# Score products of four tiles at a time in an attention stage, and three smaller moves, in a hybrid decoder block

## The chip, the cores and the metric

One Trainium2 chip, one of its cores. The metric is the device time of one execution in microseconds; the median over the runs is compared. Engines are named as in the profile: PE is TensorE's matmuls, PEld its weight loads, DVE is VectorE, ACT is ScalarE, POOL is GpSimd, SP is SyncE, whose queue issues most of the DMAs.

## What is computed

One decoder block on 1024 positions of width 1024, in float32:

```python
h = x + 0.5 * swiglu(rms_norm(x, g1), w1, w3, w2)               # D_FF = 2816
u = rms_norm(h, g)
proj = u @ w_in                       # q, k, v (3 x 768), pool input (512), two gates (2 x 1024)
# A: 12 heads of 64 in three groups, (window, dilation) = (128,1), (512,4), (2048,16):
#    causal banded attention on each residue class, blocks of 128 queries against
#    the block before and the own one; the three groups mixed by their softmax denominators
y_attn = dilated_mixture_attention(q, k, v) @ w_branch_attn
# B: trailing means over 2/4/8/16 positions minus the token, a 128x128 map per group
y_pool = multiscale_pool(pz, pool_w, pool_scale) @ w_branch_pool
h = h + (sigmoid(gA) * y_attn + sigmoid(gB) * y_pool) @ w_out
h = h + 0.5 * swiglu(rms_norm(h, g2), ...)
return rms_norm(h, final_norm)
```

## The kernel before

**Number format.** Every operand of a matmul is split in a high part (a copy on ACT, rounded to fp32r) and a low part (the difference, on DVE or POOL). A product is three matmuls: high by high, high by low, low by high (the helper `three`). The large products use a scheme of seven products for eight (`ORDER` is 1, 6, 2, 7, 5, 4, 3); the bank of product 5 is read out once and then product 3 is accumulated into it.

**Stages.** First FFN up (to about 440 us of the span), first FFN down (`Down`, to about 650), the input projection (`items`, to 1035), attention with the pool branch's product in between (1035 to about 1154), merge and output projection, second FFN up, second FFN down. In most stages the order of the instructions on each engine is the order in which the program is written (`manual_schedule`): an engine's queue is served in that order, and an instruction that waits holds up those behind it.

**Down.** 42 steps: seven products `m`, each over six pieces `s` of the inner dimension (five of two tiles, one of one). A step of two tiles is 24 matmuls (L814). Step i loads the left sums of step i + 3 (`load`, L753) and prepares the operands of step i + 2 (`begin`: `bhi`, `ahi` on ACT at L767, `blo`, `alo` on DVE or POOL at L771). Weight pieces come through a `Stream` in a fixed order (L76): a piece is loaded as soon as its place is free, and none can overtake another. Six pieces (`APART`) have places of their own, two buffers in the pool of the down stage; a piece of these is loaded when fewer than two of them are held. They are pieces 13 and 14, 22 and 23, 37 and 38 of each down product.

**Input projection.** One item k is one of the seven products of one `Mix`. In iteration k the program writes: the eviction of the item before if that was product 1 or 5; the operands of item k + 2; the product of item k (L331); the eviction of the item before if it was another product; then one step of each job in `later` that is due: rotation, turning of values, splitting of late weights, and for the two pool mixes `window` (shifted sums L1188, splits `pd_hi`, `pd_lo` at L1192 and L1193, the product `pm` at L1200 and its eviction). Evictions are at L1084 (product 1), L1091 (7), L1095 (5), L1098 (4), L1101 (3).

**Attention.** There are N = 48 slots: two pairs of heads, three groups, eight query tiles each; `slots[s]` has one or two key blocks (`blocks`). The loop runs over q, two slots each. PSUM has eight banks under two tags, "mm" and "acc", four each. A slot's scores take two "mm" banks, one for each head; the two heads' matmuls use the two halves of the rows (64x128 weights, written `64*128` in the profile) and run side by side. One step q is, in the order of the program:

- `scores(2q)` and `scores(2q+1)`: 12 matmuls, L1624
- `trans_p(q-1)`: 4, 6 or 8 transposes of the exponents, `tp`, L1671; one "acc" bank for up to 512 columns, two for more
- one or two groups of four matmuls of the pool branch (`next(fill)`, `yp`, L1763); three groups make one "acc" bank
- `values(q-2)`: 6, 9 or 12 matmuls, `o`, L1704, one "acc" bank
- DVE: `gather(q-3)` (copies of `o`, L1727), `masked` (score minus mask with a running minimum, L1642)
- the split of step q - 1's transposes: `ehi` on ACT (L1683), `elo` on DVE (L1686)
- in two steps of four, the splits of the next group's q and k (`split_ring`, ACT L1266, POOL L1267)
- `end_branches`: a finished `yp` bank times its gate, on DVE (L1777)
- `exponents` on ACT (L1651)
- `house`: among other things the factors of the first pair of heads (steps 16, 17) and `combine` for it, two advances a step in steps 18 to 21: a step of it is four transposes into an "mm" bank (`factor_rows`, `fa`, L1605), the product on DVE (L1736), the sum on POOL (L1738); the last one is ACT's copy `att` and POOL's difference.

Behind the loop come the last transposes, `ehi` and `elo`, the last values, the factors of the second pair of heads (`factors[1]`) and its `combine`.

Of the kernel before, what the change touches and what calls it, by code (L numbers as in the profile page):

```python
# [16 lines left out]
P = 128  # L17
# [8 lines left out]
HD = 64  # L26
# [20 lines left out]
class Stream:  # L47


    def __init__(self, nc, pool):  # L50
        self.nc, self.pool = nc, pool
        self.pieces, self.tiles = [], {}
        self.depth = self.n_loaded = self.n_used = self.n_back = self.end = 0
        self.apart, self.n_apart = set(), 0

    def room(self):
        if self.n_loaded in self.apart:
            return self.n_apart < 2
        return self.n_loaded - self.n_apart < self.n_back + self.depth

    def load(self):
# [76 lines left out]
def tile_block(  # L138
# [585 lines left out]
    class Down:  # L724
# [3 lines left out]
        def __init__(self, name, sums, half_tile, pair):  # L728
            self.name, self.sums, self.half_tile = name, sums, half_tile

            self.parts = pair.parts(self.place)
            self.steps = [(m, s) for m in range(len(DOWN)) for s in range(len(PAIRS))]
            self.held, self.g, self.ops, self.banks = {}, {}, {}, {}
            self.n_lo = 0
            self.last_shared = len(self.steps) - (2 if name == "f1" else len(PAIRS))
            self.right, self.apart = {}, set()
            downs.append(self)

        def size(self, i):
            js = PAIRS[self.steps[i][1]]  # L740
# [80 lines left out]
        def run(self, pool, after, tick=None):  # L821
            def half_tile(tag, n):
                return pool.tile([P, HALF], F32, tag=tag, bufs=4, name=f"{tag}_{self.name}{n}")

            self.half_tile = half_tile
            n = len(self.steps)
            done = []
            for i, (m, s) in enumerate(self.steps):
                if i < n - 2:
                    for t in range(4):  # L830
                        self.multiply(i, t)
                if i == n - 1:
# [12 lines left out]
                if s == len(PAIRS) - 1:  # L845
                    done = [(m, t) for t in range(4)]
                self.ops.pop(i - 1, None)
                if m == len(DOWN) - 1 and tick is None:
                    raws.depth = max(3, len(PAIRS) + 1 - s)
                if i == 1:  # L850
                    next(self.parts, None)
                if i + 3 < n:
                    self.load(i + 3)
                if i + 2 < n and not ahead:
                    self.begin(i + 2)
                if i in (0, 2):
                    next(self.parts, None)
                if tick is not None:
                    tick(i)
# [554 lines left out]
    with tc.manual_schedule():  # L1414
# [4 lines left out]
        for k in range(len(items) + 4):  # L1419
# [12 lines left out]
            if k - 1 in results:  # L1432
                q, m = items[k - 1]
                mixes[q].out(m, results.pop(k - 1))
                if m == 3:
                    later.append([k, mixes[q].finish()])
            for job in list(later):
                if job[0] <= k:
                    wait = next(job[1], 0)
                    job[0] = k + wait  # L1440
                    if not wait:
                        later.remove(job)
# [168 lines left out]

    T = {}

    def scores(s):
        hp, g, i = slots[s]
        u = hp * GROUPS + g
        n = blocks(g, i)
        ks = slice((i + 1 - n) * P, (i + 1) * P)
        ps = [bank("mm", f"s{s}_{a}")[:, :n * P] for a in range(2)]
        (qhi, qlo, _), (khi, klo, _) = ring[u]  # L1620
        for j, (l, r) in enumerate(three((qhi, qlo), (khi, klo))):
            for a in range(2):
                rows = slice(a * HD, (a + 1) * HD)
                pe.matmul(ps[a], l[rows, i * P:(i + 1) * P], r[rows, ks], start=(j == 0), stop=(j == 2))  # L1624
        T[s] = {"s": ps}

    def masked(s):
        hp, g, i = slots[s]
# [214 lines left out]
    def house(s):  # L1843
# [7 lines left out]
            get_stats(*slots[s - 5][:2])  # L1851
        if N // 2 + 8 <= s < N // 2 + 11:
            advance(factors[0])
        if N // 2 + 12 <= s < N // 2 + 20:
            advance(combines[0][(s - N // 2 - 12) // 4])
        if N - 32 <= s < N - 13:
            advance(first)
        if s in (N - 6, N - 5, N - 4):
# [3 lines left out]
    with tc.manual_schedule():  # L1862
# [7 lines left out]
        splits = {}  # L1870
        for q in range(N // 2):
            send()
            scores(2 * q)
            scores(2 * q + 1)
            if q == 0:
                advance(fill, 2)
            if q > 0:
                trans_p(q - 1)
                splits[q - 1] = split_p(q - 1)
                next(fill, None)  # L1880
                if q % 4 != 3:
                    next(fill, None)
            if q > 1:
                values(q - 2)
# [24 lines left out]
        load_merge(1)  # L1909
        open_w_o()  # L1910
        q = N // 2
        trans_p(q - 1)
        splits[q - 1] = split_p(q - 1)
        advance(factors[1])
# [421 lines left out]
```

## Time and profile before

| | |
|---|---|
| median of 3 runs (lowest to highest) | 1901.11 us (1900.65 to 1902.72) |
| the profiled execution | 1900.85 us, its span 1899.1 us |
| mean granted TensorE clock | 0.999 |
| attention, 1035 to 1154 us | PE 117.88 of 119.00 us busy, DVE 96.56, ACT 81.00, POOL 48.65 |

A group's row reads: line, engine, operation, tiles written <- read, shape, count, then busy time, mean duration in ns, idle time before it and what ended that. A timeline row reads: start in us, duration in us, engine, line, operation, tiles, count, and in brackets the engine's idle time before it with what ended it. A matmul's duration runs until its result is written, and the next starts long before that; so the distance of two starts says how fast matmuls follow each other, not the duration.

### The profile page before, as it was taken

Reading aid. Unit: us, or ns where it says so; the run is one execution under the profiler, and the core shown is the slowest. Engines: PE = TensorE matmul, PEld = TensorE weight load, DVE = VectorE, ACT = ScalarE, POOL = GpSimd, SP = SyncE. Lnnn points to the kernel's source line nnn. Section 1 sums busy time; section 2 is a strip of 40 time slices with the busy share of each in tenths; the row PEclk is TensorE's granted clock in tenths of the full one; section 3 lists DMA queues with packets and bytes.
Section 4 is the critical chain, followed back from the end, with each engine's and each line's share of the span. In section 5 each row is a group of like instructions: output and inputs, shape, how many; then the busy total and the mean of one; then the engine's idle time right before and its main releaser. Section 6 shows DMA issues by size and latency. Waiting matters only on the chain. (4 is left out here: it accounts for less than half of the span.)

```text
span 1899.1 us, 24689 instructions
## 1 busy us (share of the span) xinstructions
PE 1884.7 (99%) x8822; PEld 1563.3 (82%) x8822; DVE 1337.4 (70%) x1975; ACT 773.6 (41%) x1394; POOL 718.7 (38%) x533
## 2 busy tenths in 40 slices
PE   9999999999999999999999999999999999999998
PEld 8888888888788888888888888888888888888886
DVE  6776556557886777658886787787665566577867
ACT  7323323333434543334445762363333323334344
POOL 5433333331323354445545456543333333313221
PEclk9999999999999999999999999999999999999999
DMA  5254223336465526765578968644432223354654
GB/s 190 62 199 162 84 89 116 128 117 230 148 228 204 183 89 217 239 213 196 207 254 307 314 212 282 267 153 150 143 127 105 84 103 119 134 197 156 224 195 144
DMA packets 144019, 330.78 MB, mean 174 GB/s; under 512 B 17560, under 2 KB 39064, under 8 KB 142360
## 3 DMA queue, kind: packets, MB, share of 16 engines
q1 hardware_dynamic: 140152, 318.36, 48.6%
q10 hardware_dynamic: 3744, 10.85, 1.5%
q8 instruction: 69, 1.13, 0.2%
q14 instruction: 54, 0.44, 0.1%
HBM read 229.61 MB, written 99.55 MB: 173 GB/s over the span
## 5 line engine op out<-in xcount | busy, mean ns | idle before, releaser
L814 PE MATMUL d_f<-bhi_f,alo_f 128*128 128x512 f32 x616 | 240.1, 390 | 1.4 <-POOL alo_f L771 1.2
L814 PE MATMUL d_f<-bhi_f,ahi_f 128*128 128x512 f32 x616 | 240.3, 390 | 0.0
L814 PE MATMUL d_f<-blo_f,ahi_f 128*128 128x512 f32 x616 | 239.7, 389 | 0.0
L771 POOL TENSOR_TENSOR alo_f<-g_f,ahi_f 128x512 fp32r<-128x512 f32 x60 | 90.0, 1516 | 268.1 <-ACT ahi_f L767 268.1
L331 PE MATMUL u_mixm<-xhi_t_mix,wc_mixm 128*128 128x512 f32 x608 | 157.7, 391 | 0.1
L814 PEld LDWEIGHTS d_f<-bhi_f,alo_f 128*128 128x128 f32 x616 | 115.6, 188 | 26.5 <-POOL alo_f L771 2.6
L814 PEld LDWEIGHTS d_f<-bhi_f,ahi_f 128*128 128x128 f32 x616 | 115.6, 188 | 24.2 <-ACT h L415 0.5
L814 PEld LDWEIGHTS d_f<-blo_f,ahi_f 128*128 128x128 f32 x616 | 115.6, 188 | 23.9
L331 PEld LDWEIGHTS u_mixm<-xhi_t_mix,wc_mixm 128*128 128x128 f32 x608 | 113.4, 188 | 24.0 <-ACT wc_mixm L319 0.6
L331 PE MATMUL u_mixm<-xhi_b_mix,wc_mixm 128*128 128x512 f32 x456 | 120.4, 392 | 0.5 <-DVE y_m L1095 0.5
L322 POOL TENSOR_TENSOR wc_mixm<-s_mixm,wc_mixm 128x512 fp32r<-128x512 f32 x52 | 78.1, 1503 | 109.8 <-ACT wc_mixm L319 103.9
L331 PEld LDWEIGHTS u_mixm<-xhi_b_mix,wc_mixm 128*128 128x128 f32 x456 | 84.8, 188 | 18.1 <-issue 0.9
L319 ACT ACTIVATE wc_mixm<-s_mixm 128x512 fp32r<-128x512 f32 x76 | 47.0, 628 | 110.8 <-DVE s_mixm L373 53.6
L767 ACT ACTIVATE ahi_f<-g_f 128x1024 fp32r<-128x1024 f32 x84 | 81.9, 975 | 11.5 <-DMA g_f<-gs_f 11.5
L331 PE MATMUL u_mixm<-xlo_t_mix,wc_mixm 128*128 128x512 f32 x304 | 81.3, 389 | 0.0
L322 POOL TENSOR_TENSOR wc_mixm<-raw,wc_mixm 128x512 fp32r<-128x512 f32 x40 | 59.3, 1484 | 43.1 <-ACT wc_mixm L319 35.4
L2016 PE MATMUL wo<-w_o,o_hi 128*128 128x512 f32 x224 | 69.3, 390 | 0.0
L767 ACT ACTIVATE bhi_f<-s_f2w 128x512 fp32r<-128x512 f32 x55 | 32.9, 627 | 86.0 <-DVE s_f2w L789 67.1
L767 ACT ACTIVATE bhi_f<-s_f1w 128x512 fp32r<-128x512 f32 x55 | 33.1, 629 | 83.2 <-DVE s_f1w L789 69.9
L331 PEld LDWEIGHTS u_mixm<-xlo_t_mix,wc_mixm 128*128 128x128 f32 x304 | 57.1, 188 | 12.0
L771 DVE TENSOR_TENSOR alo_f<-g_f,ahi_f 128x1024 fp32r<-128x1024 f32 (+1 forms) x48 | 59.7, 1244 | 8.3 <-ACT ahi_f L767 8.3
L331 PE MATMUL u_mixm<-xlo_b_mix,wc_mixm 128*128 128x512 f32 x228 | 61.0, 389 | 0.0
(1332 smaller groups left out, 4758.9 us busy)
## 6 DMA issues: line engine op xcount, KB each, us to landing
g_f<-gs_f SPq DMA_DIRECT2D x70, 512.0 KB
gs_f<-y_f SPq DMA_DIRECT2D x88, 256.0 KB
raw<-in_w2a_dram SPq DMA_DIRECT2D x35, 512.0 KB
raw<-in_w2b_dram SPq DMA_DIRECT2D x35, 512.0 KB
gs_f<-gb_f SPq DMA_DIRECT2D x46, 256.0 KB
raw<-in_w1a_dram SPq DMA_DIRECT2D x22, 512.0 KB
raw<-in_w3a_dram SPq DMA_DIRECT2D x22, 512.0 KB
raw<-in_w1b_dram SPq DMA_DIRECT2D x22, 512.0 KB
```

Source lines behind the costliest of these rows:

```text
L319: ac.activation(w[:, 0], src, AF.Copy)
L322: eng.tensor_tensor(w[:, 1], src, w[:, 0].bitcast(F32), op=OP.subtract)
L331: pe.matmul(p, a, b, start=(start and n == 0), stop=(n == 11), skip_group_check=not start)
L767: ac.activation(hi[:, c], src, AF.Copy)
L771: eng.tensor_tensor(lo[:, d], src[:, o], hi[:, d].bitcast(F32), op=OP.subtract)
L814: pe.matmul(self.banks[m][t], l, r, start=(first and q == 0), stop=(last and q == 2))
L2016: pe.matmul(banks[m][t], l, r, start=(st == 0 and j == 0 and q == 0), stop=(st == 1 and j == 1 and q == 2))
```

## The change

Four things, none of which alters an operand.

- A step's two slots share two score banks: head a of both slots in bank a, the second slot from column 256 on. `scores(q)` now does both slots, and even steps call it for q and q + 1 (24 matmuls), odd steps not at all. Odd steps begin with a group of `yp` ahead of the transposes, and of the groups behind the transposes the second is kept only where q mod 4 is 1; step 0 has one group instead of two. The number of groups up to the end of the loop stays 42.
- `combine` of the first pair of heads moves from the ends of steps 18 to 21 to the beginnings of the odd steps 19, 21 and 23 and to the place right behind the loop, two advances each.
- A step of `window` that would fall on an iteration whose item is product 5 is put off to the next iteration.
- The extra places of the weight stream are none at first; step 8 of a down product opens two, and loads.

```diff
     def room(self):
         if self.n_loaded in self.apart:
-            return self.n_apart < 2
+            return self.n_apart < self.places
...
             downs.append(self)
+            raws.places = 0
...
                 if i + 3 < n:
                     self.load(i + 3)
+                if i == len(PAIRS) + 2:
+                    raws.places = 2
+                    raws.load()
                 if i + 2 < n and not ahead:
                     self.begin(i + 2)
...
-                    later.append([k, mixes[q].finish()])
+                    later.append([k, mixes[q].finish(), mixes[q].kind])
             for job in list(later):
-                if job[0] <= k:
+                if job[0] <= k and not (job[-1] == "pool" and k < len(items) and items[k][1] == 5):
...
-    def scores(s):
-        hp, g, i = slots[s]
-        u = hp * GROUPS + g
-        n = blocks(g, i)
-        ks = slice((i + 1 - n) * P, (i + 1) * P)
-        ps = [bank("mm", f"s{s}_{a}")[:, :n * P] for a in range(2)]
-        (qhi, qlo, _), (khi, klo, _) = ring[u]
-        for j, (l, r) in enumerate(three((qhi, qlo), (khi, klo))):
-            for a in range(2):
-                rows = slice(a * HD, (a + 1) * HD)
-                pe.matmul(ps[a], l[rows, i * P:(i + 1) * P], r[rows, ks], start=(j == 0), stop=(j == 2))
-        T[s] = {"s": ps}
+    def scores(q):
+        banks = [bank("mm", f"s{q}_{a}") for a in range(2)]
+        for s in (2 * q, 2 * q + 1):
+            hp, g, i = slots[s]
+            n = blocks(g, i)
+            ks = slice((i + 1 - n) * P, (i + 1) * P)
+            c0 = s % 2 * 2 * P
+            ps = [b[:, c0:c0 + n * P] for b in banks]
+            (qhi, qlo, _), (khi, klo, _) = ring[hp * GROUPS + g]
+            for j, (l, r) in enumerate(three((qhi, qlo), (khi, klo))):
+                for a in range(2):
+                    rows = slice(a * HD, (a + 1) * HD)
+                    pe.matmul(ps[a], l[rows, i * P:(i + 1) * P], r[rows, ks], start=(j == 0), stop=(j == 2))
+            T[s] = {"s": ps}
...
-        if N // 2 + 12 <= s < N // 2 + 20:
-            advance(combines[0][(s - N // 2 - 12) // 4])
...
             send()
-            scores(2 * q)
-            scores(2 * q + 1)
-            if q == 0:
-                advance(fill, 2)
+            if q % 2 == 0:
+                scores(q)
+                scores(q + 1)
+            elif N // 4 + 7 <= q:
+                advance(combines[0][(q - N // 4 - 7) // 4], 2)
+            if q == 0 or q % 2 == 1:
+                next(fill, None)
             if q > 0:
                 trans_p(q - 1)
                 splits[q - 1] = split_p(q - 1)
                 next(fill, None)
-                if q % 4 != 3:
+                if q % 4 == 1:
                     next(fill, None)
...
         q = N // 2
+        advance(combines[0][1], 2)
         trans_p(q - 1)
```

More of the change, by code (lines that the diff above doesn't have):

```diff
@@ L53, in __init__ @@
         self.depth = self.n_loaded = self.n_used = self.n_back = self.end = 0
-        self.apart, self.n_apart = set(), 0
+        self.apart, self.n_apart, self.places = set(), 0, 0
     def room(self):
         if self.n_loaded in self.apart:
-            return self.n_apart < 2
+            return self.n_apart < self.places
         return self.n_loaded - self.n_apart < self.n_back + self.depth
```

## The prediction

> **What bounds the kernel now.** I read the page first.
>
> ```profile
> span 1899.1 us, 24689 instructions
> PE 1884.7 (99%) x8822; PEld 1563.3 (82%) x8822; DVE 1337.4 (70%) x1975; ACT 773.6 (41%) x1394; POOL 718.7 (38%) x533
> PEclk9999999999999999999999999999999999999999
> ```
>
> The profiled execution took 1900.85 us: the span of 1899.1 and 1.75 around it; the median of the three runs is 1901.11, 0.26 above. TensorE is busy 99% of the span at a full clock, and nothing else comes near. The change alters no operand and removes no matmul (288 score matmuls before and after), so it can only remove time in which TensorE waits, or starts matmuls further apart than their columns ask. The waits, for matmuls and for weight loads (us in total, times, longest):
>
> ```profile
> PE d_f L814 <- POOL alo_f L771: 1.2, 1, 1.2
> PE u_mixm L331 <- DVE y_m L1095: 0.5, 1, 0.5
> PEld s L1624 <- DVE o L1736: 1.8, 5, 0.4
> PEld tp L1671 <- ACT e L1651: 1.1, 4, 0.3
> PEld d_f L814 <- POOL alo_f L771: 2.6, 3, 1.7
> ```
>
> The first four are 4.6 us; the fifth is the loads' side of the first, with two shorter waits beside it. The rest of what can be won is not idle time: it shows only in the starts of matmuls, so I read the timeline of PE through one attention step (q = 11, one-block tiles).
>
> ```profile
> 1082.97 0.28 PE L1704 MATMUL o<-ehi,v_in 128*128 128x256 f32 x1
> 1083.18 0.33 PE L1624 MATMUL s<-qk_hi,qk_hi 64*128 64x128 f32 x2
> 1083.34 0.28 PE L1624 MATMUL s<-qk_in,qk_hi 64*128 64x128 f32 x2
> 1083.45 0.27 PE L1624 MATMUL s<-qk_hi,qk_in 64*128 64x128 f32 x2
> ...
> 1083.79 0.28 PE L1624 MATMUL s<-qk_hi,qk_in 64*128 64x128 f32 x2
> 1084.00 0.65 PE L1671 MATMUL tp<-ident,e 128*128 128x128 f32 x4
> 1084.41 0.47 PE L1763 MATMUL yp<-xhi_t_mix,wab 128*128 128x512 f32 x1
> ...
> 1085.41 0.28 PE L1704 MATMUL o<-ehi,v_in 128*128 128x256 f32 x1
> 1085.53 0.27 PE L1704 MATMUL o<-elo,v_in 128*128 128x256 f32 x1
> ```
>
> An output matmul is followed by its like after 0.12 us (1085.41 to 1085.53), but by the first score pair after 0.21: 0.09 lost. The first score pair takes 0.16 where later ones take 0.11: 0.05 lost. The last pair is followed by the transposes after 0.21 instead of 0.11: 0.10 lost. A visit to the 64-row shape therefore costs 0.24, and there are 24 visits. In the same rows: four transposes 0.41, one group of four pool-branch matmuls (`yp`) 1.00, one pair of tiles' scores 0.82.
>
> **The change part by part.**
>
> *Scores of four tiles in every second step.* 12 of 24 visits go: 12 x 0.24 = 2.9 us. The twelve score pairs themselves stay. The new neighbours in odd steps (output to `yp`, `yp` to transposes) are all 128-row. At q = 0 the same work (four tiles, two groups of `yp`) stands ahead of the first transposes, so nothing is counted there. Bounds 1.7 (the two changes of shape at half their measured price, first pair unsaved) to 3.3.
>
> *Rows of factors (`fa`) in odd steps.* They take "mm" banks; in steps 19 to 22 the scores stood right behind them and waited for the VectorE product that empties the bank, five times, 1.8 us. Now a score group and a step's work lie between. What is late next is the masks: step 20's second bank pair was last read by step 19's masks, which stand on VectorE behind two products and the copies of step 16. From the rows below, copies take 1.31 and four masks 0.85; with two products of the size of `elo` (0.68) they end some 4.2 us into the step, and TensorE needs 4.1 for it (0.9 `fa`, two groups, transposes, values). I count 0.3 back: gain 1.5, bounds 0.8 to 1.8.
>
> ```profile
> 1067.27 0.87 PE L1671 MATMUL tp<-ident,e 128*128 128x128 f32 x6
> 1083.29 1.31 DVE L1727 COPY o<-o 64x256 f32<-64x256 f32 x2 [1.14 <-PE o L1704]
> 1084.62 0.29 DVE L1642 CUSTOM_DVE_ANT_0 e<-s,mask 128x128 f32<-128x128 f32 x1
> 1085.47 0.68 DVE L1686 TENSOR_TENSOR elo<-tp,ehi 128x512 fp32r<-128x512 f32 x1
> 1118.28 0.32 PE L1624 MATMUL s<-qk_hi,qk_hi 64*128 64x128 f32 x1 [0.27 <-DVE o L1736]
> ```
>
> *Transposes against exponents.* ScalarE runs a loop: transposes of step q, `ehi`, ring splits (L1266) in two steps of four, exponents, transposes of step q+1.
>
> ```profile
> 1084.69 0.60 ACT L1683 ACTIVATE ehi<-tp 128x512 fp32r<-128x512 f32 x1 [0.78 <-PE tp L1671]
> 1085.18 1.14 ACT L1266 ACTIVATE xlo_b_mix<-xhi_b_mix 128x512 fp32r<-128x512 f32 x2
> 1087.38 0.39 ACT L1651 ACTIVATE e<-e,own_stats 128x128 f32<-128x128 f32 x1
> 1086.21 0.33 PE L1624 MATMUL s<-xlo_b_mix 64*128 64x128 f32 x2
> 1087.09 1.16 PE L1671 MATMUL tp<-ident,e 128*128 128x128 f32 x4
> 1088.00 0.95 PE L1763 MATMUL yp<-xhi_b_mix,wab 128*128 128x512 f32 x3
> ```
>
> Here the transposes came 3.09 after the last ones and took 0.91 instead of 0.41: the loop wants 3.6 with ring splits (2.45 without). That short step, q mod 4 = 3 with one group of `yp`, is where the four waits of 1.1 lie. Afterwards the transposes of an even step come behind four tiles' scores, 0.8 later than now, so those waits go. But from an even step to an odd one there is now transposes 0.41, a group 1.00, values 0.80 (1085.41 to 1086.21), a group 0.93 = 3.14. Without ring splits that is enough; with them it lacks 0.45 at q = 10, and for tiles of one and two blocks (six transposes are 0.22 longer, 0.63; three more values at 0.12) 3.72 against some 3.9 (two exponents of double width), 0.2 each at q = 6 and 14; at q = 18 the `fa` cover it. Net 1.1 - 0.9 = 0.2 gained, bounds -1.2 to +1.1.
>
> *Accumulator banks in odd steps.* A group ahead of the transposes can end one `yp` bank and the next group open another, while two-bank transposes hold two: the values' bank is then free only after `elo`. Counting groups, this happens at q = 3 and 15 with one group between. `elo` ends 2.15 after the transposes' start (1084.00 to 1086.15); with six transposes and one group the values are due 1.63 after it. Two times 0.4 = 0.8 lost, bounds 0 to 1.6.
>
> *The end of attention.* The second half of the factor work for hp 0 is now behind the loop: four `fa` ahead of the last transposes, one product, one POOL sum, and ScalarE's `att` copy waiting for it in front of the last `ehi`. The same products and sums stood in step 21 before, so the work is no extra. The last `ehi`, and the factors of hp 1 behind it, come late by at most a product and a POOL sum, 0.7 + 1.75 = 2.45 by the rows of `elo` above and `alo_f` below; transposes, a group and values (0.41 + 1.00 + 0.80) run meanwhile. 0.5 lost, bounds 0 to 1.2.
>
> *Pooling steps off fifth results.*
>
> ```profile
> 991.72 1.37 DVE L1193 TENSOR_TENSOR pd_lo<-pw,pd_hi 128x512 fp32r<-128x512 f32 x1 [0.68 <-ACT pd_hi L1192]
> 993.01 0.68 DVE L1095 TENSOR_TENSOR y_m<-u_mixm,y_m 128x512 f32<-128x512 f32 x1
> 993.83 1.17 PE L331 MATMUL u_mixm<-xhi_b_mix,wc_mixm 128*128 128x512 f32 x4 [0.50 <-DVE y_m L1095]
> ```
>
> A pooling step emitted with product 5 (`pd_lo`, itself held 0.68 by ScalarE) stands on VectorE ahead of that product's eviction (L1095), and product 3 accumulates into the same bank. Following the order of jobs, five pooling steps fall on a fifth product and only the last made TensorE wait. Moved one item on, it stands behind the eviction. Gain 0.5; below nothing (-0.5) if it then holds up another eviction. All pooling shifts by one to three items, far from the ring loads that need it; the `h` buffers suffice.
>
> *Later extra weight places.*
>
> ```profile
> 462.64 1.41 SPq L76 DMA_DIRECT2D raw<-in_w2a_dram  x3
> 465.29 13.95 SPq L753 DMA_DIRECT2D g_f<-gs_f  x4
> 473.16 1.06 ACT L767 ACTIVATE ahi_f<-g_f 128x1024 fp32r<-128x1024 f32 x1 [4.86 <-DMA g_f<-gs_f]
> 474.30 3.50 POOL L771 TENSOR_TENSOR alo_f<-g_f,ahi_f 128x512 fp32r<-128x512 f32 x2 [9.04 <-ACT ahi_f L767]
> 477.86 0.51 PE L814 MATMUL d_f<-bhi_f,alo_f 128*128 128x512 f32 x1 [1.23 <-POOL alo_f L771]
> GB/s 31 0 0 62 282 313 304 222 297 346 381 393 236 211 326 417 411 138 18 7 0 193 304 195 7 171 295 0 138 328 0 0 0 0 42 370 55 15 0 0
> raw<-in_w2a_dram SPq DMA_DIRECT2D x35, 512.0 KB
> ```
>
> Three weight blocks are issued at 462.64; two of them are the extra ones, 1 MB, and step 7's left sums queue behind. The GB/s row (455 to 500 us, 1.1 us a slice) shows 200 to 400 until 475 and long empty slices after 478. At 350 GB/s 1 MB is 3 us: the sums land by about 470 instead of 473.1, POOL ends near 475, and its reader, due at 476.5, no longer waits. Gain 1.4 (1.23 idle and the slow restart), and 0.2 for a like delay in the second FFN, whose wait is one of the short ones in the loads' row (2.6 in all, 1.7 the longest): 1.6, bounds 0 to 1.8. Issued in step 8 (about 482.7, behind that step's own load on SP), the blocks meet an almost idle queue and are wanted three steps of 5.4 us later; the sums behind them on SP are wanted in step 10. Cover: 10 us; cost 0.
>
> **Sum.** -2.9 - 1.5 - 0.2 + 0.8 + 0.5 - 0.5 - 1.6 = -5.4 us, so 1895.45 on the profiled execution's scale, 1895.7 on the median's.
>
> **Rivals.** One measurement of this kernel can tell about 0.2%, 3.8 us.
>
> *Given back in the odd steps.* The loop and bank costs at their upper bounds: gain 5.4 - 1.4 - 0.8 - 0.7 = 2.5, time 1898.6. For it: the odd interval of 3.14 is already under the loop's 3.6. Against: only two steps of four carry ring splits.
>
> *The exponent loop sets every odd step; slower.* Without loop, bank and end costs the gains are 2.9 + 1.8 + 1.1 + 0.5 + 1.6 = 7.9. If each of the 11 odd steps from q = 3 on lacked 1.1 us, 12.1 would be lost and the time were 1905.3. It decides from 0.72 a step. Against: without splits the loop wants 2.45 and gets 3.14.
>
> *Masks wait for the whole bank.* Two tiles now share a bank, so a guard by bank holds the first tile's mask for the second tile's scores (1083.45 to 1083.79 and more: 0.4). The copies at 1083.29 keep VectorE until 1084.60, behind both tiles, so I count 0. Were that cover gone, 11 odd steps would lose 0.4 each: 4.4 back, 1900.1. The Trainium skill, "PSUM — Partial Sum Buffer", section "PSUM bank collisions raise a hardware error", has this as its rule: guard PSUM by bank and quadrant, not by address, since another column of the same bank still collides. By that rule the wait must exist; no run here shows its price yet.
>
> *The extra blocks were not what delayed the sums.* The 1.6 stays: 1897.3.
>
> *The saving in shape does not come.* If the 0.24 follows each pair of tiles rather than each visit, 2.9 goes: 1898.6. The rows speak against it: between 1083.45 and 1083.79 the second tile's pairs keep 0.11.
>
> **How the numbers follow.** Forecast 0.68 (own range 1893.2 to 1897.3), given back 0.10, shape saving absent 0.05, masks 0.03, blocks not the cause 0.08, loop slower 0.06. Faster by over 0.2% (below 1897.3): 0.68 and half of the 0.08, 0.72. Within: 0.10 + 0.05 + 0.03 + 0.04 = 0.22. Slower: 0.06. The range runs from just above all gains without costs (1893.2) to past the two cases at 1898.6: 1893.4 to 1899.0.
>
> **What would show it.** Right: no wait of `s` for L1736 and none of `d_f` for `alo_f`; L1095 gone from TensorE's waits; 12 bursts of 24 score matmuls; waits of `tp` for `e` moved to q = 7, 11 and 15. Wrong: waits of `tp` in most odd steps, of `o` for `elo` beyond q = 3 and 15, a new wait for weights in steps 10 to 12 of the down products, or 0.2 us still lost between tiles inside a burst.

## The result and the profile after

The changed kernel takes 1893.89 us, the median of 6 runs (1892.93 to 1895.22), against 1900.58 of the kernel before in the same comparison: 0.9965 of its time, 95% interval 0.9953 to 0.9976, so 6.7 us less. The forecast was 1895.7, in a range from 1893.4 to 1899.0. The profiled execution took 1894.76 us, its span is 6.1 shorter than that of the kernel before. One run behind the table of experiments below (factor rows at even ends) took 3796.86 us, twice the others; its ratio leaves it out, and the median without it is 1894.47.

The page after, the lines that answer to those of before:

```profile
span 1893.0 us, 24691 instructions
PE 1880.3 (99%) x8822; PEld 1562.5 (83%) x8822; DVE 1334.7 (71%) x1975; ACT 773.2 (41%) x1394; POOL 713.3 (38%) x533
PEclk9999999999999999999999999999999999999999
```

The same 8822 matmuls at the same full clock. TensorE's waits (total, times, longest), first those of matmuls and then one of the weight loads:

```profile
PE o L1711 <- DVE o L1734: 1.6, 1, 1.6
PE o L1711 <- DVE elo L1693: 0.3, 1, 0.3
PE tp L1678 <- ACT e L1658: 0.2, 1, 0.2
PEld tp L1678 <- ACT e L1658: 2.1, 8, 0.4
```

TensorE's waits of `d_f` for `alo_f`, of `u_mixm` for L1095 and of `s` for the product are gone, as foreseen (on the loads' side one of 0.4 for `alo_f` is left, in the second FFN down). In the first row stands one that was not: the values, for the copies of a gather. (Lines of the attention stage are higher by 4 to 7 in the changed kernel: `s` is L1631, `tp` L1678, `o` L1711, the product L1743.)

Where the time went is read from the distance of two starts of TensorE in the two timelines, the first matmul of one stage to the first of the next where the table says nothing else:

| stage, us | before | after | difference | forecast |
|---|---|---|---|---|
| first FFN down, first to last matmul | 215.61 | 213.83 | -1.8 | -1.4 |
| input projection | 379.90 | 379.28 | -0.6 | -0.5 |
| attention, first score to first merged output | 118.34 | 115.11 | -3.2 | -3.3 |
| merge to second FFN up | 101.86 | 101.95 | +0.1 | 0 |
| second FFN down, first to last matmul | 209.66 | 209.52 | -0.1 | -0.2 |
| behind the last matmul | 8.64 | 8.17 | -0.5 | 0 |

The last two rows are no merit of the change. Over all profiles of this study the last lies between 7.2 and 8.8, in no order that follows the edits; the second FFN down takes 209.24 to 209.66 in the four profiles without the new weight places and 209.21 to 209.52 in those with them. For that reason the experiments on attention are compared by this stage's length first and by the whole time second.

Within attention the score product now comes in bursts. TensorE's timeline in step 6 (four tiles, of one and two blocks):

```profile
1059.18 0.28 PE L1711 MATMUL o<-ehi,v_in 128*128 128x256 f32 x1
1059.39 0.33 PE L1631 MATMUL s<-xlo_b_mix 64*128 64x128 f32 x2
...
1060.07 0.28 PE L1631 MATMUL s<-xlo_b_mix,xhi_b_mix 64*128 64x256 f32 x2
1060.18 0.22 PE L1631 MATMUL s<-xlo_b_mix 64*128 64x128 f32 x2
...
1060.76 0.28 PE L1631 MATMUL s<-xlo_b_mix,xhi_b_mix 64*128 64x256 f32 x2
1060.96 0.87 PE L1678 MATMUL tp<-ident,e 128*128 128x128 f32 x6
```

Between the second and the third tile (1060.07 to 1060.18) lies the ordinary 0.11; the 0.21 into and the 0.20 out of the 64-row shape are paid once for four tiles.

### The profile page after: what moved, and what is told of

It reads as the page before. It is cut to its first block, busy times and chain, and to the rows that moved or that the text cites. A ratio compares the mean times of both kernels' runs of the same rounds, so it can differ in the third digit from the quotient of the medians.

```text
span 1893.0 us, 24691 instructions
## 1 busy us (share of the span) xinstructions
PE 1880.3 (99%) x8822; PEld 1562.5 (83%) x8822; DVE 1334.7 (71%) x1975; ACT 773.2 (41%) x1394; POOL 713.3 (38%) x533
## 3 DMA queue, kind: packets, MB, share of 16 engines
q8 instruction: 70, 1.15, 0.3%
## 4 chain that ended last, share of the span: by engine, by line
PE 55%; DVE 2%; ACT 2%; issue 1%; POOL 0%; DMA 0%; ACTq 0%; SPq 0%; DVEq 0%; POOLq 0%
PE u_mixm L331 15%; PE d_f L815 8%; PE wo L2025 4%; PE yp L1770 2%; PE ya L1836 1%; PE o L1711 1%; PE u_f20b L331 1%; PE u_f21a L331 1%; PE u_f210b L331 1%; PE u_f210a L331 1%; PE u_f29b L331 1%; PE u_f29a L331 1%; PE u_f28b L331 1%; PE u_f28a L331 1%; PE u_f27b L331 1%; PE u_f27a L331 1%
```

## The experiments

Each took the kernel before or the changed one and altered one thing. The first column of numbers is the median and its ratio to the kernel before with the 95% interval, the second the length of attention in the profile.

| | time, us | ratio | attention, us |
|---|---|---|---|
| attention of the change alone | 1897.53 | 0.9981 (0.9972 to 0.9990) | 116.37 |
| weight places alone | 1899.08 | 0.9991 (0.9982 to 1.0000) | 118.30 |
| pooling order alone | 1900.66, one run | | 118.30 |
| change, `combine` as before | 1894.07 | 0.9964 (0.9952 to 0.9977) | 115.10 |
| change, bursts split | 1898.29 | 0.9988 (0.9980 to 0.9997) | 119.60 |
| shared banks alone | 1898.81 | 0.9988 (0.9980 to 0.9997) | 116.35 |
| change, last factor rows later | 1896.63 | 0.9979 (0.9970 to 0.9988) | 115.37 |
| the same, filled step 0, spread splits | 1899.94 | 0.9996 (0.9987 to 1.0005) | 118.57 |
| change, factor rows at even ends | 1894.64 | 0.9969 (0.9958 to 0.9981) | 115.45 |
| change, filled step 0, later splits | 1893.33 | 0.9963 (0.9951 to 0.9975) | 114.42 |
| both | 1894.73 | 0.9968 (0.9956 to 0.9980) | 114.49 |
| both, `att` copy last | 1893.30 | 0.9963 (0.9949 to 0.9976) | 114.12 |

### The three parts, each alone

Attention alone: the changed kernel with the weight stream and the order of the pooling jobs put back. Places alone and pooling alone: those two edits made to the kernel before. The lines that tell them apart are these of the change:

```diff
# places
-            return self.n_apart < 2
+            return self.n_apart < self.places
# pooling
-                if job[0] <= k:
+                if job[0] <= k and not (job[-1] == "pool" and k < len(items) and items[k][1] == 5):
```

> The kernel before with the attention part of the change alone (shared banks, bursts of 24 score matmuls, the moved factor rows); weight places and pooling steps as before. Theory: the parts add up, so the attention stage shortens by 3.2 us as between the two profiles (118.34 to 115.11 from the first score to the first ya matmul) and the time by about the same, 1897.4; the waits of d_f for alo_f (1.2) and of u_mixm for L1095 (0.5) are still there. Rival: what attention wins depends on the earlier transfers being out of the way; then the stage shortens by less than 2 us here.

> The kernel before with the later extra weight places alone. Theory: the two extra blocks ahead of step 7's left sums delayed them; the g_f wait of 4.86 us on ScalarE shrinks by about 3 us, the wait of d_f for alo_f goes, the first down product shortens by 1.4 to 1.8 us (215.61 to about 213.9), the second by 0.2, the time to about 1899.0. Rival: the sums wait for a free buffer or for the queue of earlier stores and not for the blocks; then the g_f wait and the 1.2 us stay.

> The kernel before with the put-off pooling steps alone; to be read in the trace, since half a microsecond is below what the times tell. Theory: the projection stage (379.90 from its first to the first score matmul) shortens by 0.5 to 0.6 and PE waits for L1095 no more. Rival: the VectorE work put off holds up another eviction, and the stage stays within 0.2 of 379.90.

Places (the whole time alone would not show it, its interval reaches 1): the first down stage is 213.88 us against 215.61 and the wait of `d_f` is gone. The chain that was argued from the sums' arrival shows in the timeline: ScalarE's copy for which TensorE waited in the end stood idle 4.86 us for its sums before and started at 473.16; now it is idle 0.93 and starts at 469.89 (470 was forecast). The copy behind it is idle 1.23, for which TensorE does not wait:

```profile
469.89 1.06 ACT L768 ACTIVATE ahi_f<-g_f 128x1024 fp32r<-128x1024 f32 x1 [0.93 <-DMA g_f<-gs_f]
473.13 1.06 ACT L768 ACTIVATE ahi_f<-g_f 128x1024 fp32r<-128x1024 f32 x1 [1.23 <-DMA g_f<-gs_f]
476.04 0.94 SPq L76 DMA_DIRECT2D raw<-in_w2a_dram  x2
```

The extra blocks are issued at 476.04, behind everything the sums need. Pooling: the projection takes 379.02 against 379.90, and TensorE has no wait left in it.

Attention alone shortened its stage by 2.0 and not by 3.2, within what the rival said. (The whole time fell by 3.1, but this profile has 7.43 us behind the last matmul against 8.64 before.) The missing 1.26 is one wait in step 3, which in the changed kernel is 0.32 and which the two other parts do not have:

```profile
1048.61 0.63 ACT L1266 ACTIVATE xlo_b_mix<-xhi_b_mix 128x512 fp32r<-128x512 f32 x1 [0.48 <-DMA xhi_b_mix<-qk]
1050.41 1.06 ACT L1686 ACTIVATE ehi<-tp 128x512 fp32r<-128x512 f32 x2
1051.77 0.39 PE L1707 MATMUL o<-ehi,v_in 128*128 128x256 f32 x1 [1.56 <-DVE elo L1689]
```

ScalarE waits for a transfer of q and k, `ehi` stands behind it in its queue, and the values wait for `elo`. The kernel before has the same late transfer (idle 0.39 and 0.65) but with TensorE still behind; in the changed kernel the split starts without idle time at 1045.45. So the parts are not quite independent: what the transfer queues do in the stage ahead decides whether these 1.3 us are lost. Why the two other edits bring the transfer in time was not separated; in the profile of either alone it is.

### Banks without bursts, and bursts taken apart

The first is the kernel before with two tiles a bank (`scores(q)` as in the change); the second is the changed kernel with the transposes moved between the two halves of a burst:

```diff
# banks alone (kernel before)
-            scores(2 * q)
-            scores(2 * q + 1)
+            scores(q)
# bursts split (changed kernel), even steps
                 scores(q)
+                if q > 0:
+                    trans_p(q - 1)
                 scores(q + 1)
...
             if q > 0:
-                trans_p(q - 1)
+                if q % 2 == 1:
+                    trans_p(q - 1)
```

> The kernel before with one thing of the change: two tiles of scores share a bank, so that a step takes two banks and not four; no bursts, the factor rows by slot as before. Theory: the waits of the factor rows for a bank (1.8 us in the kernel before, for the masks of the step) mostly go, the 24 visits stay, waits for exponents stay: attention 116.5 to 117.3 us against 118.3, time 1899.1 to 1899.9. Rival one, the banks shift the same wait to the next step's scores: attention 118.0 to 118.8, time as before, 1900.6. Rival two, the masks of a first tile wait until the second tile of its bank is written: then the masks start after the 12th matmul of a visit, not after the 6th, about 0.6 us later in each step, and the waits of the transposes for the exponents grow by a part of that in the steps where they show: attention 119 to 121.

> The changed kernel, but in each even step the transposes of the last pair stand between the first and the second pair of tiles of scores, so that the scores are again 24 visits of 12 matmuls and not 12 of 24; banks, combine and places stay as changed. Theory, the change of tile shape costs about 0.24 us per visit: 12 more visits cost about 2.9 us, and the transposes, now 1.3 us later behind the exponents, lose the waits of 0.2 to 0.4 us at steps 7 and 11 that the changed kernel's trace shows only where they stood in even steps (none), so nothing is relieved: attention from the first score to the first merged output about 118.0 us against 115.1, the time about 1896.8. Rival, the shape has no price of its own and the bursts were worth something because of the order of the work: attention within 0.5 us of 115.1, time 1893.9 +- 0.5. Between the two, 116 to 117, a part of the price is per visit and a part is not.

To price them, all starts of the stage were summed by what stands on either side of them, less 0.4167 ns a column. This deduction was chosen for the table and is no measured price; it is the same for the same matmul, so it drops out of differences; it makes the row "between scores" negative, since two score matmuls run side by side.

| us, starts less columns | before | banks alone | after | bursts split |
|---|---|---|---|---|
| into a run of scores | 2.55 | 2.55 | 1.13 | 2.88 |
| out of it | 2.82 | 2.82 | 1.40 | 2.71 |
| between scores | -1.25 | -4.39 | -4.97 | -4.31 |
| between transposes | 8.82 | 9.90 | 9.01 | 8.93 |
| `yp` to values | 0.36 | 0.37 | 2.86 | 3.11 |
| all else | 9.26 | 9.32 | 9.89 | 10.49 |

Banks alone: attention is 2.0 shorter, and the scores wait for no bank any more, which is worth 3.1 (-1.25 to -4.39). Of this 2.6 lie in the steps with the factor rows and 0.5 in step 0, where the second tile no longer needs a bank of its own; the transposes, reached earlier, wait 1.1 longer for exponents. The theory held, with a gain a little above its range (116.35 against 116.5 to 117.3), and the first rival fell. So sharing the banks is enough to end the waits behind the factor rows: here these stand where they stood before. The second rival's mechanism exists but costs nothing in step 0. VectorE's mask and the last score pairs ahead of it, in step 0, first in the kernel before and then with shared banks:

```profile
1035.80 0.28 PE L1624 MATMUL s<-qk_hi,qk_in 64*128 64x128 f32 x2
1036.24 0.28 DVE L1642 CUSTOM_DVE_ANT_0 e<-s,mask 128x128 f32<-128x128 f32 x1
```

```profile
1036.12 0.28 PE L1627 MATMUL s<-qk_hi,qk_in 64*128 64x128 f32 x2
1036.52 0.28 PE L1627 MATMUL s<-qk_hi,qk_in 64*128 64x256 f32 x2
1036.84 0.29 DVE L1645 CUSTOM_DVE_ANT_0 e<-s,mask 128x128 f32<-128x128 f32 x1 [0.19 <-PE s L1627]
```

The first tile's mask followed its own scores after 0.16; with a shared bank it comes 0.44 after them, 0.04 after the second tile's. That is what the Trainium skill, "PSUM — Partial Sum Buffer", section "PSUM bank collisions raise a hardware error", demands: guard by bank (and quadrant), not by address. The runs show the wait; they do not show whether it was needed. In step 0 it costs nothing because the exponents start 2.89 us after the first scores in both kernels, behind other work of ScalarE, above all the loading of a table (`ACT_TABLE_LOAD`), and in the changed kernel too (rows of ScalarE there, where the first scores start at 1033.19):

```profile
1034.68 1.28 ACT L1465 ACT_TABLE_LOAD   x1
1036.08 0.39 ACT L1658 ACTIVATE e<-e,stats 128x128 f32<-128x128 f32 x1
```

From step 3 on the copies of a gather keep VectorE as long, as the prediction counted.

From banks alone to the changed kernel, 12 runs of scores go: -1.42 into, -1.42 out, -0.58 between, 3.4 us. A further 0.7 is hidden in the row "between transposes": the first two transposes start 0.164 apart behind scores and 0.109 behind a `yp`, in every step, and 12 runs of transposes less follow scores. That makes 4.1 us, 0.34 a run. Taken apart again, 11 runs cost 3.7 us (1.75 + 1.31 + 0.66), and 0.3 more where `yp` no longer follow transposes; attention is 4.5 longer. The rival that the bursts gain by order alone is out. The theory's mechanism stands, and its price of 0.24 was too low. TensorE's timeline of the split kernel:

```profile
1060.96 0.87 PE L1678 MATMUL tp<-ident,e 128*128 128x128 f32 x6
1061.76 0.33 PE L1631 MATMUL s<-xlo_b_mix 64*128 64x128 f32 x2
...
1062.44 0.28 PE L1631 MATMUL s<-xlo_b_mix,xhi_b_mix 64*128 64x256 f32 x2
1062.64 0.50 PE L1770 MATMUL yp<-xhi_t_mix,wab 128*128 128x512 f32 x1
1062.98 0.87 PE L1770 MATMUL yp<-xlo_t_mix,wab 128*128 128x512 f32 x3
```

The last transpose starts at 1061.56 and the scores 0.20 behind it, where transposes follow each other at 0.11: the way in costs 0.09, as from values. What the prediction's sum lacks comes behind the way out: the second `yp` starts 0.34 behind the first, where later ones follow at 0.23, just as the second transpose comes late behind scores. Of the 4.5 another 0.25 is a wait of the values for `elo` in step 15, and the rest are small distances around `yp`. What it is in the 64-row shape that costs (the array's form, its weight loads or the pairs) no run separates.

### The factor rows put back

The changed kernel with `combine` of the first pair of heads at the ends of steps 18 to 21 again, nothing of it behind the loop.

```diff
+        if N // 2 + 12 <= s < N // 2 + 20:
+            advance(combines[0][(s - N // 2 - 12) // 4])
...
-            elif N // 4 + 7 <= q:
-                advance(combines[0][(q - N // 4 - 7) // 4], 2)
...
-        advance(combines[0][1], 2)
         trans_p(q - 1)
```

> The changed kernel, but with the factor rows of the first pair of heads at the ends of steps 18 to 21 as before. Theory: the one new long wait of the changed kernel (1.6 us behind the loop, values waiting for the copies L1734) comes from the factor product, its POOL sum and ScalarE's att copy having been put in front of the last transposes; without them it goes, and with bursts the score banks are used a step apart, so at most 0.5 us of the old wait for the products (1.8) comes back: attention 113.5 to 114.2 us, time 1.0 to 1.6 below the changed kernel, about 1892.5. Rival: moving the factor rows to the odd steps is what took the 1.8 us away; then that wait returns in full, the time is level with the changed kernel or above it.

The theory fell. The wait at the end went, and one of 1.11 came back in front of step 22's second pair of tiles (VectorE and TensorE, in order of time):

```profile
1125.93 0.60 PE L1609 MATMUL fa<-ident,f_of 128*128 128x128 f32 x4
1127.92 0.68 DVE L1743 TENSOR_TENSOR o<-o,fa 128x512 f32<-128x512 f32 x1
1128.65 0.38 PE L1631 MATMUL s<-xlo_b_mix 64*128 64x256 f32 x1 [1.11 <-DVE o L1743]
```

The product that empties the bank stood behind masks, `elo` and a gate product on VectorE, and the burst right behind the factor rows wants all four banks. Moving the factor rows to the odd steps is thus worth what it costs at the end, and no more: 115.10 against 115.11.

### What the end of attention waits for

In the changed kernel the values of the last step but one wait 1.57 us. All engines there, TensorE's pool groups and transfers left out:

```profile
1134.50 0.68 DVE L1784 TENSOR_TENSOR gb<-yp,gb 128x512 f32<-128x512 f32 x1
1135.09 0.68 DVE L1743 TENSOR_TENSOR o<-o,fa 128x512 f32<-128x512 f32 x1
1135.91 1.29 POOL L1745 TENSOR_TENSOR o<-o,o 128x512 f32<-128x512 f32 x1 [3.44 <-DVE top L1580]
1136.10 1.17 DVE L1582 TENSOR_TENSOR w<-top,stats 128x48 f32<-128x48 f32 x1
1137.19 0.85 DVE L1734 COPY o<-o 64x256 f32<-64x256 f32 x2
1138.19 0.36 PE L1711 MATMUL o<-ehi,v_in 128*128 128x256 f32 x1 [1.57 <-DVE o L1734]
```

The values need the bank that the copies of a gather (1137.19) empty. On VectorE ahead of those stand the moved product and the second pair's factor operations, one of which, on 48 columns, takes 1.17 us; it ends when GpSimd's sum does. Several ways were tried to take that away. First, the last two advances of `combine` moved from in front of the last transposes to behind the last gather:

```diff
         q = N // 2
-        advance(combines[0][1], 2)
         trans_p(q - 1)
...
         gather(q - 1)
+        advance(combines[0][1], 2)
         for n in range(8):
```

> The changed kernel with the last factor rows of the first head pair (two steps of its combine) taken from in front of the last transposes to behind the last gather, ahead of the second pair's. Theory: the wait of 1.6 us of the last values for a bank came from the product and the factor operations that stood ahead of the copies of a gather on VectorE, and goes with them: attention 113.3 to 113.8 us against 115.1, time about 1892.4. Rival, the moved product is then late for what follows it (the second pair's products and the merges stand behind it on VectorE and GpSimd): the wait comes back in front of the second pair's factor rows or the first merged output, attention 114.6 to 115.5, time 1893.6 to 1894.3.

```profile
1135.32 0.21 DVE L1582 TENSOR_TENSOR w<-top,stats 128x48 f32<-128x48 f32 x1
1136.44 0.36 PE L1711 MATMUL o<-ehi,v_in 128*128 128x256 f32 x1 [0.20 <-DVE o L1734]
1140.93 2.00 ACT L1600 ACTIVATE f_of<-f 128x1024 f32<-128x1024 f32 x2 [4.99 <-PE fa L1609]
1142.04 0.66 PE L1609 MATMUL fa<-ident,f_of 128*128 128x128 f32 x4 [1.15 <-ACT f_of L1600]
```

The first half of the theory held: the operation takes 0.21 and the values wait 0.20. The rival won all the same, by a mechanism it had not named: the second pair's factors are written to the one buffer that the first pair's rows are read from (`f_of`, one buffer), so ScalarE stood 4.99 us until the last row was read. Factor rows then waited 1.15, and the first merged outputs 0.84 and 0.23 for `att`: attention 115.37 and the stage behind it 104.12 against 101.95.

Second, the same with two more edits, against the waits of the transposes. One moves a pool group from step 1 to step 0, so that each has two (the expectations say "both pooling groups", which is one too many); the other spreads the splits of q and k, one a step over four steps in place of two a step over two.

```diff
             if q == 0 or q % 2 == 1:
-                next(fill, None)
+                advance(fill, 2 if q == 0 else 1)
...
-                if q % 4 == 1:
+                if q % 4 == 1 and q > 1:
                     next(fill, None)
...
             if i > 1 and 0 < u < len(uses) - 1:
-                split_ring(uses[u + 1], i - 2)
-                split_ring(uses[u + 1], i)
+                split_ring(uses[u + 1], 2 * (i - 2))
+            if i < 2 and u > 1:
+                split_ring(uses[u], 2 * i + 1)
```

> A version made from the findings: the changed kernel, with the last factor rows of the first head pair moved behind the last gather (as in b4), with both pooling groups of step 1 given to step 0 in front of the first transposes, and with the splits of the ring spread one per step over four steps in place of two per step over two. Theory: beside the 1.6 us of b4 the waits of the transposes at step 1 (0.7 us) and at steps 7, 11 and 15 (about 0.9 us together, where two ring splits stand ahead of the exponents on ScalarE) go: attention 111.7 to 112.5 us, time about 1891. Rival one, as in b4 the end's wait comes back: 113.3 to 114, time about 1892.4. Rival two, the ring splits that come later make the next group's first scores wait for them, 0.3 to 1 us in each of 3 groups: attention 113 to 115.

```profile
1126.86 1.27 POOL L1271 TENSOR_TENSOR xhi_b_mix<-xhi_b_mix,xlo_b_mix 128x512 fp32r<-128x512 f32 x1
1128.18 0.39 PE L1631 MATMUL s<-xhi_b_mix,xlo_b_mix 64*128 64x256 f32 x2 [0.96 <-POOL xhi_b_mix L1271]
```

All waits of transposes went, so their reason is shown, but the last split came too late for the burst that reads it, five times and 3.2 us in all (rival two, dearer than it said), and the end lost as in the kernel before it.

Third, the factor rows spread so that none is left for the end (`spread` advances each half that it is given by one step), then the two edits on the transposes in a milder form: the pool group moved as above, and of the two steps with splits, only in the first do they stand behind the exponents; then both together.

```diff
+        ODD, EVEN = {19: (0,), 21: (0, 1), 23: (1, 1)}, {18: (0,), 20: (0,), 22: (1,)}
...
             elif N // 4 + 7 <= q:
-                advance(combines[0][(q - N // 4 - 7) // 4], 2)
+                spread(ODD[q])
...
             house(2 * q + 1)
+            spread(EVEN.get(q, ()))
...
         q = N // 2
-        advance(combines[0][1], 2)
         trans_p(q - 1)
# splits, moved from in front of exponents(2 * q) where i is 2
             exponents(2 * q + 1)
+            if late_split:
+                split_ring(uses[u + 1], i - 2)
+                split_ring(uses[u + 1], i)
```

> The changed kernel with the factor rows of the first head pair spread so that none is left for the end: one group at the end of the even steps 18, 20 and 22, where no scores follow, one at the start of step 19, two at the starts of 21 and 23. The order at the end is otherwise as in the kernel before. Theory: the wait of 1.6 us of the last values goes, because no product or sum of the first head pair stands near the last gathers, and the single buffer of the factors is free in time for the second pair, which it was not when the same work was moved behind the gathers: attention 113.3 to 113.9 us against 115.1, the stage behind it 101.9 as in the changed kernel, time about 1892.3. Rival: a product at the end of an even step holds up the masks or the copies of the next on VectorE, and the second factor rows of the odd step wait for the bank: 0.5 to 1.5 us back, attention 114 to 115.1, time 1892.9 to 1893.9.

> The changed kernel with two edits against the waits of the transposes: both pooling groups of step 1 stand in step 0, ahead of the first transposes, and in the first of the two steps with ring splits these stand behind the exponents on ScalarE and no longer ahead of them; their number per step stays. Theory: the waits of the transposes at step 1 (0.7 us) and at steps 7, 11 and 15 (0.27, 0.65, 0.27) go, and no scores wait for a split, since the last splits of a group stand where they stood: attention 113.3 to 113.8 us against 115.1, time about 1892.4. Rival: the splits behind the exponents hold up the next copy of the transposes, and the values behind it wait by as much as was won: attention 114.6 to 115.3, time 1893.4 to 1894.

> Both together: factor rows spread over steps 18 to 23 with none at the end, both pooling groups of step 1 in step 0, ring splits of the first of their two steps behind the exponents. Theory: the two gains lie at different places and add up: attention 111.7 to 112.5 us against 115.1, time about 1890.8. Rival: they meet in steps 18 to 20, where ring splits of the last group, products of the factor rows and masks come together, and 0.5 to 1 us is given back: attention 112.5 to 113.3, time about 1891.5.

The spread failed. Two sums now queue on GpSimd in step 23, and ScalarE's `att` copy waits for them ahead of `ehi` and the exponents:

```profile
1131.14 2.67 POOL L1745 TENSOR_TENSOR o<-o,o 128x512 f32<-128x512 f32 x2 [6.28 <-DVE o L1743]
1133.84 0.63 ACT L1750 ACTIVATE att<-o 128x512 fp32r<-128x512 f32 x1 [3.25 <-POOL o L1745]
1135.98 1.80 PE L1678 MATMUL tp<-ident,e 128*128 128x128 f32 x7 [1.06 <-ACT e L1658]
```

The 1.6 of the end were exchanged for some 2.0 in the last transposes: attention 115.45, above theory and rival. The edits on the transposes won 0.7 of the 1.3 to 1.8 expected: none of their waits is left, but a burst waits for a split (0.48 idle at 1082.78) and the values of steps 3 and 15 wait for `elo` by 0.2 more each. Both together took 114.49, with the waits of both (+0.34 and -0.69 against the changed kernel would have made 114.76).

Last, in that version, the `att` copy alone moved behind step 23:

```diff
-        ODD, EVEN = {19: (0,), 21: (0, 1), 23: (1, 1)}, {18: (0,), 20: (0,), 22: (1,)}
+        ODD, EVEN = {19: (0,), 21: (0, 1), 23: (1,)}, {18: (0,), 20: (0,), 22: (1,)}
...
         q = N // 2
+        spread((1,))
         trans_p(q - 1)
```

> The version with factor rows spread over steps 18 to 23, pooling groups of step 1 in step 0 and later ring splits (d2), with one thing moved: the last step of the first head pair's second half, in which ScalarE copies the sum and waits for GpSimd, stands behind step 23 and no longer at its start. Theory: in d2 the last transposes waited 1.9 us in all for exponents that stood on ScalarE behind this copy, which itself waited 3.25 us for two sums on GpSimd (in d1's trace); with the copy behind the exponents that wait goes and the one of 1.6 of the changed kernel doesn't return, since no product stands at the end: attention 112.5 to 113.0 us against 114.5 of d2 and 115.1, time about 1891.8. Rival: the end of the attention has about 1.7 us too little work for TensorE in whatever order, and the wait moves again, to the last values or to the second pair's factor rows: attention 114 to 114.6, time 1893.3.

```profile
1134.77 1.30 POOL L1751 TENSOR_TENSOR att<-o,att 128x512 fp32r<-128x512 f32 x1 [2.08 <-ACT att L1750]
1134.94 1.19 DVE L1582 TENSOR_TENSOR w<-top,stats 128x48 f32<-128x48 f32 x1
1136.06 0.85 DVE L1734 COPY o<-o 64x256 f32<-64x256 f32 x2
1137.05 0.36 PE L1711 MATMUL o<-ehi,v_in 128*128 128x256 f32 x1 [1.18 <-DVE o L1734]
```

The wait of the transposes went, as the theory said, and the values wait again, as the rival said: with no product ahead of the copies, but with the small operation at 1.19, this time beside GpSimd's difference. At 114.12 this is the shortest attention of the study, 1.0 below the changed kernel; the time, 1893.30, can't be told from the 1893.89 of the change.

## Why the prediction was right, and where its steps were not

The direction came out, and every stage within 0.5 us. The time came out 1.8 us below the forecast of 1895.7: the kernel before measured 1900.58 and no longer 1901.11, 0.5 of the gain lies behind the last matmul, where nothing was forecast, and the rest is within what the runs differ by. Inside attention the sum of -3.3 was right to 0.1 by errors that cancel, which is luck. Term by term, from the table of starts:

- **Scores in bursts**: forecast -2.9, measured -4.1 (0.7 of it between transposes). The step that was too small is the price of a visit, 0.24: it was read at q = 11, the cheapest kind, and without the 0.05 that the transposes behind the scores lose. A first pair of 256 columns loses 0.10, one of 128 loses 0.05. (The lower bound of 1.7 does not follow from its own words: half of 0.19 without the first pair, twelve times, is 1.1.)
- **Factor rows**: forecast -1.5, measured -2.6, but not by the step that was named: the shared banks alone win all of it, without the move to the odd steps. The term took TensorE's idle time, 1.8, for the whole price; each wait also slows the starts behind it. The 0.3 that the masks were to give back did not come. Another 0.5 came from step 0, where the prediction counted nothing.
- **Transposes against exponents**: forecast -0.2, measured +0.8 (waits of 1.1 before, 1.9 after). The waits of the changed kernel lie where they were put, at steps 7, 11 and 15, with 0.27, 0.65 and 0.27 against 0.2, 0.45 and 0.2. One more, 0.7, lies in step 1: "the same work (four tiles, two groups of `yp`) stands ahead of the first transposes, so nothing is counted there" counted the work and not its length: with the 0.5 of step 0's bank gone, the same work is over sooner (the first transposes came 4.35 us after the first scores before, at 1039.87, and come after 3.72 now, at 1036.91), and step 0's exponents, behind ScalarE's table load, are not.
- **Accumulator banks**: 0.8 forecast for steps 3 and 15, measured 0.50 and 0.25 there. (The forecast's rows, 2.15 against 1.63, make 0.52 a step and not 0.4.)
- **The end of attention**: 0.5 forecast with bounds 0 and 1.2, measured 1.75 in the starts, 1.57 of it idle. This is the step that failed most. It followed the moved work to ScalarE, where `ehi` was to come late, and did not look at what the product and GpSimd's sum do to VectorE, where the copies that empty the bank stand behind them. Of the 1.57 about 0.96 is the small operation's growth from 0.21 to 1.17 (an estimate by these two rows), and the product's 0.68 covers the rest.
- All other starts, +0.6: small distances at the new neighbours of `yp`, not counted.

**Places**: -1.6 forecast, -1.4 of it in the first down stage, where -1.8 was measured; alone the edit gave -1.7 there. The 0.2 forecast for the second FFN is not shown: its stage varies by more than that without the edit. **Pooling**: -0.5 forecast, -0.6 in the change and -0.9 alone.

Of the rivals, the loop of the exponents did not become the bound in the odd steps: three of eleven waited, none by over 0.7. The saving in shape came. The mask does wait for the whole bank, and the wait cost nothing that shows.

## What to carry to other kernels

A price read from one instance should be read from the dearest and the cheapest one: the visit at q = 11 was of the cheapest kind among 24. When work is moved, follow it on every engine that it touches to the next instruction that empties a buffer, above all where a buffer is single: four orders of the same factor work each turned the end's wait into another, of 1.1 to 2 us. And price a wait by the distance of starts around it, not by its idle time.

## What the runs showed of the hardware

The same VectorE operation, L1582 in the changed kernel (L1578 in the kernel before), on 128x48 with both inputs in SBUF, takes 0.21 us in the nine profiles in which GpSimd is idle then, and 1.17 to 1.19 in the five in which GpSimd runs a 128x512 sum or difference, and it ends within 0.1 of that; VectorE's copies and masks, which read PSUM, keep their time beside GpSimd's sums. The Trainium skill, "GPSIMD Engine Reference", section "1. Specifications", says that GpSimd shares its SBUF interfaces with VectorE and that they contend when a VectorE instruction has two SBUF inputs; these fourteen profiles agree, and give the price: the small operation waits for the rest of the large one. That taking GpSimd's operation away from there would bring the time back was not tried by itself.
